# A float32 two-stack kernel: the S5 preparation cut into fine pieces, and the mixer's rotations and outputs placed elsewhere

## The chip, the core and the metric

The kernel runs on one core of a Trainium2 chip. The metric is the device time of the program in microseconds (us), from one launch; lower is better. Five engines of the core matter here: PE (TensorE, matrix products, results in PSUM), DVE (VectorE, elementwise work), ACT (ScalarE, activations, casts and copies), POOL (GpSimd, a second elementwise engine that also issues some DMAs) and SP (SyncE, which issues most DMAs). Each engine works through its own list of instructions in the order of that list.

## The reference

The input is one sequence of 256 positions of width 1024. A first stack has two layers, a second stack (attention, a dense feed-forward part, attention again, a mixture of experts) follows; the change touches only the first. Of that:

```python
h = x
for i in range(2):
    f = swiglu(rmsnorm(h, ...), ffn1_w_gate[i], ffn1_w_up[i], ffn1_w_down[i])
    h = h + 0.5 * rmsnorm(f, ...)
    m = mixer(rmsnorm(h, ...), ...);  h = h + rmsnorm(m, ...)
    ...                                    # ffn2, of the form of ffn1

def s5_branch(u, ...):                     # a part of the mixer
    lam_bar = jnp.exp(lam * step)          # 64 groups x 64 states, complex
    b_bar = ((lam_bar - 1.0) / lam)[..., None] * lax.complex(b_re, b_im)
    bu = jnp.einsum("blgc,gnc->blgn", ug, b_bar)
    # states[t] = lam_bar * states[t-1] + bu[t]
    y = jnp.real(jnp.einsum("blgn,gcn->blgc", states, c)) + d_skip * u
    val, gate = jnp.split(jax.nn.gelu(y) @ w_glu, 2, axis=-1)
    return val * jax.nn.sigmoid(gate)
```

The mixer projects its input with one wide matrix, sends parts of the result through a chunked state-space branch (SSD) and through the S5 branch, gates both, adds them and projects again. `swiglu` is `(silu(x @ w_gate) * (x @ w_up)) @ w_down` with a hidden width of 2816. All is float32.

## The kernel before

**Weights.** Every weight matrix is streamed from HBM in tiles of 128 x 1024 float32, called units here (512 KB each). SP issues the load into one of four raw buffers; ACT casts the tile to a rounded float32 form, `hi` (line 1576); DVE takes the difference `lo` (line 1577, "the split"); PE then makes three products for each pair of blocks: hi with hi, hi with lo, lo with hi (lines 1585 to 1593). The pairs of `hi` and `lo` rotate through a ring of three, lengthened in some stages by space that is free there (named `big`, `part` and `more` in the profile). `stream_b` keeps the weight block in the array and streams 256 positions (24 matmuls of 256 columns for a unit), `stream_k` keeps the input and streams 512 columns of the weights (12 matmuls for a unit). A feed-forward part has 66 units: six column blocks, c0 to c5, each with its gate and its up units, then 22 units of the down product, d0 to d21. The first block goes through `lead_b`, which runs its first five splits without waiting for the norm.

**Order of the work.** A tile scheduler decides each engine's list from its own estimates of time. The author binds it in places with `issue_after(x)`, which puts an instruction behind `x` on the engine of `x`. `self.last_lo` is the last split (on DVE), `self.last_mm` the last product of a unit (on PE), `self.last_pow` the reciprocal root of a norm (on POOL).

**The S5 preparation** runs beside ffn1, as a generator (`prep`) that is advanced at named places. It computes the step, the exponentials, sines and cosines of the recurrence (`mix_prep`, layer 0 only, some hundred DVE instructions on 128 x 64), a table of coefficients FL, then for each of four quarters q: POOL multiplies the input matrix B by powers (`s5_wb`, lines 341 to 344), DVE multiplies C by FL (`s5_ct`, lines 372 to 377, result s5CF), PE, ACT and DVE make the block matrices of the recurrence within four positions (`s5_products`, lines 396 to 414, PSUM tile zfa). For each half of 16 groups `s5_powers_prep` builds a table of 63 powers of a complex number by doubling (lines 301 to 303): for n = 1, 2, 4, ..., 32 two pairs of products, a difference and a sum, each on 16 groups x min(n, 63 - n) elements. In layer 0 both halves are built in ffn1; those of layer 1 are built in ffn2 of layer 0, at the units d2 and d8. The table `PREP` names the places at which the generator is advanced (its first list) and the products are made (its second), by column blocks c and down units d; each advance is bound behind the last split and behind the last norm's root.

**The mixer** (`mixer_body`) works through the list `ORDER`: p0 to p3 are four projection groups (eight units each, with a short convolution on DVE, line 569), d the step sizes of SSD (a chain of some 35 DVE instructions on 32 x 256, lines 585 to 604), g0 to g3 gates (four units each, accga to accgd), c0 to c3 the SSD cores, o0 to o3 the S5 outputs: 48 small matmuls (zoa to zod), then on ACT and DVE the gelu (`s5_gelu`, lines 504 to 509, and 515 to 559). Behind ORDER come the S5 gated product (`glu`, accgl), which needs all four outputs, and the two branch products. The S5 recurrence itself (`s5_rec`) rotates the states by the table of powers, scans them and rotates them back, for two halves of the groups: 14 DVE steps for a half (12 products, differences and sums of 128 x 1024, line 545, and two scans, line 549), 28 in all. It is `self.side`; `beside()`, which `stream_b` calls behind each split, advances it by one step. All 28 must be through before o0. The tables of the second half are loaded into the buffers of the first.

Of the kernel before, what the change touches and what calls it, by code (L numbers as in the profile page):

```python
# [30 lines left out]
ORDER = "p0 d p1 g0 g1 o0 o1 p2 c0 g2 c1 p3 o2 o3 g3 c2 c3".split()  # L31
# [4 lines left out]
    "X": [2, 3, 0, 1], "U": [4, 5], "A": [12, 13, 6, 7, 8, 9, 10, 11, 12, 13, 6, 7, 8, 9, 6, 7], "M": [15, 16],  # L36
# [42 lines left out]
class Mixer:  # L79
# [58 lines left out]
    def mix_prep(self, I):  # L138
# [67 lines left out]
        mag = self.exp32(cut, xr, P, NL)  # L206
        sn, cs = self.sincos32(cut, th, NL)

# [25 lines left out]
        cmul(*L[2], L[1], L[1])  # L234
        cmul(*L[3], L[2], L[1])
        cmul(*L[4], L[2], L[2])

# [6 lines left out]
        v.tensor_scalar_mul(lin, lim, -1.0)  # L244
        cmul(*f, (num, L[1][1]), (lre, lin))
        v.tensor_tensor(f[0], f[0], den, op=ALU.mult)
        v.tensor_tensor(f[1], f[1], den, op=ALU.mult)

        self.FL = ct.tile([P, 3, 4, NL], F32, name="FL")
        fi = t("fli")  # L250
        for d in range(4):
# [7 lines left out]
            v.tensor_scalar_mul(self.FL[:, 2, d, :], self.FL[:, 0, d, :], -1.0)  # L259

# [3 lines left out]
        cmul(*u2, (cs, sn), (cs, sn))  # L264
        cmul(self.s4dir[:, 0], self.s4dir[:, 1], u2, u2)
        v.tensor_tensor(mag, mag, mag, op=ALU.mult)
        v.tensor_tensor(self.s4len, mag, mag, op=ALU.mult)

# [12 lines left out]
    def s5_powers_prep(self, l, h):  # L281


        g = self.nc.gpsimd
        tt = self.nc.vector.tensor_tensor
        Ed = self.Ed[l, h] = self.dram.tile([3, P, 1024], F32, tag="Ed", name=self.nm("Ed"), bufs=4)
        if True:
            E = [self.slot("B", "E").rearrange("p (a i) -> p a i", i=64) for _ in range(3)]
            Et = self.slot("B", "Et").rearrange("p (k a i) -> p k a i", k=2, i=32)
            x, y = Et[:, 0], Et[:, 1]  # L290
            ls = slice(l * 32 + h * 16, l * 32 + h * 16 + 16)
            g.memset(E[2][:, :, 0], 0.0)
            self.nc.scalar.copy(E[2][:, :, 1:], self.s4len[:, ls].unsqueeze(2).to_broadcast([P, 16, 63]))
            for r in range(2):
# [9 lines left out]
            for r in range(3):  # L304
                g.dma_start(Ed[r], E[r].rearrange("p a i -> p (a i)"))
# [1683 lines left out]
```

## Time and profile before

| quantity | value |
|---|---|
| device time of three runs | 2931.49, 2934.55, 2935.66 us (median 2934.55) |
| profiled execution | time 2936.55 us, span 2934.5 us |
| mean granted PE clock | 0.981 of full speed |
| busy over the span | PE 2814.3 us (96%), DVE 2181.6 (74%), ACT 1674.2 (57%), POOL 206.0 (7%) |
| ffn1, mixer and ffn2 of layer 0 (accumulators) | 11.9 to 240.7, 247.7 to 662.5, 663.8 to 852.6 us |
| ffn1 and mixer of layer 1 | 855.3 to 1056.6, 1059.8 to 1473.8 us |

The profile is of one execution, 2.0 us above the median of the three runs. The span is the time from its first to its last instruction; all stages follow one another, because each needs the hidden state of the one before. A busy PE is not a PE at its peak, so each stage has to be read with its granted clock. Idle time of an engine is put down to whatever released it last.

### The profile page before, as it was taken

How to read it: one execution, taken by the hardware profiler on the slowest of the kernel's cores; microseconds unless marked ns; L12 is line 12 of the kernel's file. 1: busy time of each engine (PE TensorE's matmuls, PEld its weight loads, DVE VectorE, ACT ScalarE, POOL GpSimd, SP SyncE). 2: the span in 40 equal slices, each digit the busy share in tenths (PEclk: the TensorE clock that was granted, in tenths of full speed). 3: DMA queues.
4: the chain of work that ended last, by engine and by line, in shares of the span. 5: the costliest groups of instructions: out<-in, count | busy, mean ns of one | idle time of the engine just before them, and what ended most of it. 6: DMA issues, size and time to landing. Idle time of an engine off the chain costs nothing. (4 is left out here: it accounts for less than half of the span.)

```text
span 2934.5 us, 49144 instructions
## 1 busy us (share of the span) xinstructions
PE 2814.3 (96%) x19040; PEld 2508.2 (85%) x19040; DVE 2181.6 (74%) x3043; ACT 1674.2 (57%) x2389; POOL 206.0 (7%) x257
## 2 busy tenths in 40 slices
PE   8979999999999999999999999999999999999997
PEld 7968888999979888888999898987678888888886
DVE  5886877765667758777755566555589999999997
ACT  5434456545445444475554445445377777777776
POOL 2140001000004100010000000000000000000000
PEclk9999999999999999999999999999899999999998
DMA  7677565576567775656855646654589999999993
GB/s 238 199 250 242 160 204 164 197 227 188 184 223 249 241 221 174 194 155 196 264 171 180 215 154 192 186 192 132 184 279 356 343 361 361 343 359 356 354 344 145
DMA packets 350928, 687.88 MB, mean 234 GB/s; under 512 B 32672, under 2 KB 121952, under 8 KB 350688
## 3 DMA queue, kind: packets, MB, share of 16 engines
q1 hardware_dynamic: 336592, 637.42, 65.9%
q0 software_dynamic: 13952, 46.74, 4.8%
q8 instruction: 151, 2.47, 0.3%
q14 instruction: 89, 0.73, 0.1%
q10 hardware_dynamic: 144, 0.52, 0.0%
HBM read 658.05 MB, written 26.54 MB: 233 GB/s over the span
## 5 line engine op out<-in xcount | busy, mean ns | idle before, releaser
L1577 DVE TENSOR_TENSOR lo<-raw,hi 128x1024 fp32r<-128x1024 f32 x646 | 788.6, 1230 | 296.8 <-ACT hi L1576 285.1
L1576 ACT CAST hi<-raw 128x1024 fp32r<-128x1024 f32 x646 | 674.9, 1048 | 455.6 <-PE accmo L1587 84.6
L1586 PE MATMUL accmo<-lo,xg 128*128 128x512 f32 (+1 forms) x768 | 289.7, 378 | 2.3 <-DVE lo L1577 2.3
L1587 PE MATMUL accmo<-hi,xg 128*128 128x512 f32 (+1 forms) x768 | 285.2, 372 | 0.0
L1585 PE MATMUL accmo<-hi,xg 128*128 128x512 f32 (+1 forms) x768 | 274.0, 373 | 1.4 <-ACT hi L1576 1.4
L1577 DVE TENSOR_TENSOR big<-raw,big 128x1024 fp32r<-128x1024 f32 x147 | 184.9, 1259 | 110.2 <-ACT big L1576 109.3
L1576 ACT CAST big<-raw 128x1024 fp32r<-128x1024 f32 x147 | 153.7, 1049 | 168.0 <-issue 31.1
L1577 DVE TENSOR_TENSOR part<-raw,part 128x1024 fp32r<-128x1024 f32 x111 | 135.3, 1223 | 85.5 <-ACT part L1576 83.1
L1576 ACT CAST part<-raw 128x1024 fp32r<-128x1024 f32 x111 | 116.1, 1050 | 114.2 <-DMA raw<-in_ffn_w_gate_dram 17.4
L1586 PEld LDWEIGHTS accmo<-lo,xg 128*128 128x128 f32 x768 | 144.6, 188 | 32.3 <-DVE lo L1577 5.6
L1585 PEld LDWEIGHTS accmo<-hi,xg 128*128 128x128 f32 x768 | 144.6, 188 | 28.1 <-ACT hi L1576 2.6
L1587 PEld LDWEIGHTS accmo<-hi,xg 128*128 128x128 f32 x768 | 144.8, 189 | 22.5
L1586 PE MATMUL accmo<-lo,th 128*128 128x512 f32 x352 | 138.0, 392 | 0.0
L1587 PE MATMUL accmo<-hi,th 128*128 128x512 f32 x352 | 137.7, 391 | 0.0
L1577 DVE TENSOR_TENSOR lo<-big,hi 128x1024 fp32r<-128x1024 f32 x88 | 106.6, 1223 | 10.7 <-ACT hi L1576 7.6
L1585 PE MATMUL accmo<-hi,th 128*128 128x512 f32 x352 | 109.2, 391 | 0.0
L1576 ACT CAST hi<-big 128x1024 fp32r<-128x1024 f32 x88 | 92.7, 1054 | 27.0 <-PE accmo L1587 26.7
L1592 PE MATMUL accfa<-xh,lo 128*128 128x256 f32 x352 | 99.8, 284 | 0.0
L1591 PE MATMUL accfa<-xh,hi 128*128 128x256 f32 x352 | 99.7, 283 | 0.0
L1593 PE MATMUL accfa<-xl,hi 128*128 128x256 f32 x352 | 99.7, 284 | 0.0
L1577 DVE TENSOR_TENSOR lo<-more,hi 128x1024 fp32r<-128x1024 f32 x68 | 82.3, 1223 | 7.0 <-ACT hi L1576 5.0
L1576 ACT CAST hi<-more 128x1024 fp32r<-128x1024 f32 x68 | 71.4, 1053 | 19.3 <-PE accmo L1587 17.8
(993 smaller groups left out, 8603.3 us busy)
## 6 DMA issues: line engine op xcount, KB each, us to landing
raw<-in_w_gu_moe_dram SPq DMA_DIRECT2D x190, 512.0 KB, 5.3
raw<-in_w_in_dram SPq DMA_DIRECT2D x128, 512.0 KB, 4.4
raw<-in_w_down_moe_dram SPq DMA_DIRECT2D x94, 512.0 KB, 5.6
raw<-in_ffn_w_gate_dram SPq DMA_DIRECT2D x88, 512.0 KB, 4.1
raw<-in_ffn_w_up_dram SPq DMA_DIRECT2D x88, 512.0 KB, 4.3
raw<-in_ffn_w_down_dram SPq DMA_DIRECT2D x88, 512.0 KB, 4.2
big<-in_w_gu_moe_dram SPq DMA_DIRECT2D x60, 512.0 KB, 5.7
more<-in_w_gu_moe_dram SPq DMA_DIRECT2D x46, 512.0 KB, 5.7
```

The costliest lines, as they stand in the source:

```text
L1576: nc.scalar.copy(hi, raw)
L1577: self.last_lo = nc.vector.tensor_tensor(lo, raw, hi.bitcast(F32), op=ALU.subtract).ins
L1585: mm(ps, lh, rh, start=first, stop=False)
L1586: mm(ps, lh, rl, start=False, stop=False)
L1587: self.last_mm = mm(ps, ll, rh, start=False, stop=last).ins
L1591: mm(ps, lh, rh, start=first, stop=False)
L1592: mm(ps, ll, rh, start=False, stop=False)
L1593: self.last_mm = mm(ps, lh, rl, start=False, stop=last).ins
```

## The change

1. `PREP`, `product` and the binding to `last_pow` are gone. ffn1 sets `self.side = self.prep(...)` behind its first column block (layer 0) or its second (layer 1), and `beside()` advances it by one piece behind every split; `stream_k` now calls `beside()` too. The generator has many more yields: 48 pieces in layer 0 and 31 in layer 1, behind 58 and 50 splits. The rest, if there is any, runs at the end of the stage.
2. `s5_powers_prep` is called once for a layer, in ffn1 of that layer (layer 1 leaves ffn2). It builds 32 powers for all 32 groups of the layer, and ACT then copies them into tables for each half, whose middle is the power zero: once as they are, once reversed with the sign of the imaginary part turned. The first product by `jm` in `s5_products` moves from DVE to ACT.
3. In the mixer, `proj` sets `pace` to 2 except in p2, so that a rotation follows every second split there. ORDER puts p2 and g2 ahead of o0, g3 between c0 and c1. The lists of buffers X and A serve the new order.

```diff
-ORDER = "p0 d p1 g0 g1 o0 o1 p2 c0 g2 c1 p3 o2 o3 g3 c2 c3".split()
+ORDER = "p0 d p1 g0 g1 p2 g2 o0 o1 c0 g3 c1 p3 o2 o3 c2 c3".split()
 MIXER = {
-    "X": [2, 3, 0, 1], "U": [4, 5], ...
+    "X": [2, 3, 0, 1, 0] + [2, 3, 1, 0] * 5, "U": [4, 5], ...
...
-PREP = (
-    ("c0 c1 c2 c3 c4 d0 d3 d6 d9 d12".split(), "d0 d4 d10 d15".split()),
-    ("c1 c2 c4 d1 d6".split(), "c4 d1 d6 d11".split()),
-)
...
-    def s5_powers_prep(self, l, h):
+    def s5_powers_prep(self, l):
+        E = [self.slot("B", "E").rearrange("p (a i) -> p a i", i=32) for _ in range(2)]
...
+        for n in (1, 2, 4, 8, 16):
+            k = min(n, 31 - n)
+            b = [e[:, :, n : n + 1].to_broadcast([P, 32, k]) for e in E]
+            for r, op in ((0, ALU.subtract), (1, ALU.add)):
+                tt(x[:, :, :k], E[0][:, :, 1 : k + 1], b[r], op=ALU.mult)
+                if n > 8:
+                    yield
+                tt(y[:, :, :k], E[1][:, :, 1 : k + 1], b[1 - r], op=ALU.mult)
+                tt(E[r][:, :, n + 1 : n + 1 + k], x[:, :, :k], y[:, :, :k], op=op)
...
+        for h in range(2):
+            F = [self.slot("B", "Eh").rearrange("p (a i) -> p a i", i=64) for _ in range(3)]
+            for r in range(2):
+                g.memset(F[r][:, :, 0], 0.0)
+                cp(F[r][:, :, 32:], E[r][:, hs])
+                self.nc.scalar.activation(F[r][:, :, 1:32], E[r][:, hs, :0:-1], AF.Copy, scale=1.0 - 2.0 * r)
...
     def s5_products(self, q, p0, bq, CF, s):
-        nc.vector.tensor_scalar_mul(T, K, self.jm[:, 0:1])
+        nc.scalar.activation(T, K, AF.Copy, scale=self.jm[:, 0:1])
...
     def beside(self):
+        self.beat += 1
+        if self.beat % self.pace:
+            return
         with self.tc.issue_after(self.last_lo):
             next(self.side, None)
...
         def proj(g):
+            self.pace = 1 if g == 2 else 2
             pr[g] = self.ssd_proj(W, l, g, xh, xl)
+            self.pace = 1
...
     def stream_k(self, w, xh, xl, nk, order=None, aside=None):
             u = self.unit(w[k0 * P : (k0 + kk) * P, :], kk, D)
+            self.beside()
...
-                if aside:
-                    aside(f"d{i}")
...
     def ffn1(self, I, l, xT):
         def aside(w):
             if w == f"c{l}":
                 self.ring_drop((6, 7), (8, 9))
-            if w in at[1]:
-                self.product()
-            if w in at[0]:
-                with self.tc.issue_after(self.last_lo), self.tc.issue_after(self.last_pow.ins):
-                    next(steps, None)
+                self.side = self.prep(I, l)
```

DVE's list at the very start of the program, before (`big` and `lo` are splits, `xn` is the normed first half of the input, `xl` the low part of its transpose, `sm` a sum of the norm):

```order
L1747 SCALAR_TENSOR_TENSOR sm_122<-sm_116,sm_119 128x1
L1771 SCALAR_TENSOR_TENSOR xn_126<-h_99,sm_123,gn_114 128x512 x2
L1747 SCALAR_TENSOR_TENSOR sm_149<-sm_143,sm_146 128x1
L1771 SCALAR_TENSOR_TENSOR xn_153<-h_100,sm_150,gn_114 128x512 x2
L1577 TENSOR_TENSOR big_170<-raw_177,big_170 128x1024
L1720 TENSOR_TENSOR xl_113<-tr_128,xh_112 128x4x128
```

The same place after the change:

```order
L1775 SCALAR_TENSOR_TENSOR sm_122<-sm_116,sm_119 128x1
L1606 TENSOR_TENSOR big_170<-raw_177,big_170 128x1024
L1606 TENSOR_TENSOR big_170<-raw_187,big_170 128x1024
L1606 TENSOR_TENSOR lo_199<-raw_197,hi_198 128x1024
L1606 TENSOR_TENSOR lo_211<-raw_209,hi_210 128x1024
L1799 SCALAR_TENSOR_TENSOR xn_126<-h_99,sm_123,gn_114 128x512 x2
L1606 TENSOR_TENSOR lo_225<-raw_223,hi_224 128x1024
```

Four splits have moved ahead of the first normed half, and a fifth ahead of the second one. On ACT, the fifth cast (`hi_224`) likewise stands ahead of the squares of the second half and of every cast of a transposed input. On POOL, 14 DMA issues of the preparation, seven of which wait for earlier DMAs to land, have moved ahead of the first root of the norm.

DVE's list in the down product of ffn1, layer 0, before (L301 to L303 powers, L372 to L377 C times FL, L404 to L414 products):

```order
L410 TENSOR_TENSOR s5u_1607<-s5u_1607,dd_1802 128x8x16
L374 TENSOR_TENSOR s5CF_1827<-s5CF_1827,s5u_1828 128x8x64
L303 TENSOR_TENSOR E_1889<-Et_1892 128x16x8
L412 TENSOR_SCALAR s5u_1607<-s5u_1607,jm 128x512
L404 TENSOR_TENSOR dd_1990<-delta,sd 128x128
L376 TENSOR_TENSOR s5u_1828<-s5c_1602,FL 128x512
L1577 TENSOR_TENSOR big_170<-raw_2018,big_170 128x1024
```

The products of the first quarter after the change:

```order
L1606 TENSOR_TENSOR big_170<-raw_1905,big_170 128x1024
L426 TENSOR_TENSOR dd_1943<-delta,sd 128x128
L436 SCALAR_TENSOR_TENSOR s5u_1552<-s5u_1552,jm 128x8x48
L436 SCALAR_TENSOR_TENSOR s5u_1552<-s5u_1552,jm 128x8x32
L1606 TENSOR_TENSOR big_170<-raw_1965,big_170 128x1024
L388 TENSOR_TENSOR s5CF_1780<-s5c_1547,FL 128x8x64
L392 TENSOR_TENSOR s5CF_1780<-s5c_1547,FL 128x8x64
L436 SCALAR_TENSOR_TENSOR s5u_1552<-s5u_1552,jm 128x8x16
L1606 TENSOR_TENSOR lo_2002<-raw_2000,hi_2001 128x1024
```

Up to twelve instructions of three different strands stood between two splits before; now two or three stand there.

PE's list at the end of the last S5 output in the mixer of layer 0 (zod), before:

```order
L494 MATMUL zod_5344<-s5T_5341,U_3158 64x4x16
L495 MATMUL zod_5344<-s5CF_5340,S_2763 64x4x16
L496 MATMUL zod_5344<-s5CF_5340,S_2763 64x4x16
L1591 MATMUL accgd_5415<-xh_2478,hi_5420 128x256
L1592 MATMUL accgd_5415<-xh_2478,lo_5421 128x256
```

And after:

```order
L516 MATMUL zod_5442<-s5T_5439,U_3125 64x4x16
L517 MATMUL zod_5442<-s5CF_5438,S_2730 64x4x16
L518 MATMUL zod_5442<-s5CF_5438,S_2730 64x4x16
L1620 MATMUL accgl_5754<-g_632_4547,hi_5757 128x256
L1621 MATMUL accgl_5754<-g_632_4547,lo_5758 128x256
```

The 96 matmuls of the gate g3 (accgd) that stood behind zod have moved ahead of it, to the first outputs; the gated product accgl follows at once. It begins with the outputs 0 and 1; 48 of its matmuls stand ahead of the first transpose of output 2 in both lists.

## Rows read from the trace of the kernel before

**Rows 1.** The page, busy time of each engine over the span.

```profile
PE 2814.3 (96%) x19040; PEld 2508.2 (85%) x19040; DVE 2181.6 (74%) x3043; ACT 1674.2 (57%) x2389; POOL 206.0 (7%) x257
```

**Rows 2.** Stages: length; busy PE, PEld, DVE, ACT, POOL; granted clock; DMA.

```profile
12.00:100.00 88.00, 86.63 (x611) 81.48 (x611) 60.96 (x134) 47.87 (x66) 12.12 (x25) 1.00 0.71 218
100.00:246.00 146.00, 122.35 (x905) 107.36 (x904) 127.82 (x250) 56.00 (x78) 51.60 (x47) 0.94 0.76 243
...
337.00:402.00 65.00, 55.39 (x407) 53.84 (x406) 61.57 (x83) 24.71 (x38) 3.06 (x6) 0.89 0.59 189
...
476.00:530.00 54.00, 48.07 (x506) 42.85 (x504) 37.62 (x66) 34.93 (x70) 6.02 (x7) 0.97 0.42 134
...
663.00:853.00 190.00, 189.38 (x1258) 174.47 (x1257) 123.08 (x191) 93.04 (x129) 7.34 (x18) 1.00 0.66 205
853.00:1058.00 205.00, 200.17 (x1509) 182.59 (x1506) 140.50 (x165) 97.85 (x137) 51.68 (x40) 0.99 0.73 233
```

**Rows 3.** Waits of PE, 100 to 246 us: total, times, longest.

```profile
PE zfa L396 <- DVE s5CF L374: 7.5, 1, 7.5
PE trfa L1730 <- DVE xn L1771: 5.2, 1, 5.2
PE accfa L1586 <- DVE lo L1577: 4.4, 1, 4.4
PE accfa L1591 <- DVE ht L1827: 2.8, 1, 2.8
```

**Rows 4.** Waits of PE, 337 to 402 us (p1, g0, g1 of layer 0).

```profile
PE accgb L1592 <- DVE lo L1577: 3.2, 2, 2.3
PE accpb L1592 <- DVE lo L1577: 2.6, 1, 2.6
PE accga L1591 <- ACT zs L642: 2.3, 1, 2.3
```

**Rows 5.** DVE, busy time of the powers alone (tile Et), 12 to 246 us.

```profile
12.00:246.00 234.00, 29.69 (x72) 0.96 0.74 233
```

**Rows 6.** DVE by shape, 100 to 246 us: busy, mean ns, idle before.

```profile
L375 DVE TENSOR_TENSOR s5CF<-s5c,FL 128x512 f32<-128x512 f32 x4 | 5.0, 1240 | 0.0
...
L376 DVE TENSOR_TENSOR s5u<-s5c,FL 128x512 f32<-128x512 f32 x4 | 2.7, 682 | 0.0
...
L412 DVE TENSOR_SCALAR s5u<-s5u,jm 128x512 f32<-128x512 f32 x4 | 1.9, 479 | 0.0
```

**Rows 7.** The start, instructions in order of time: start us, us.

```profile
9.90 1.05 ACT L1576 CAST big<-raw 128x1024 fp32r<-128x1024 f32 x1 [1.47 <-DMA raw<-in_ffn_w_gate_dram]
...
11.93 0.79 PE L1585 MATMUL accfa<-big,xh 128*128 128x512 f32 x1
...
14.07 5.57 SPq L1571 DMA_DIRECT2D raw<-in_ffn_w_up_dram  x4
...
17.45 2.92 POOL L199 DMA_DIRECT2D sd<-in_s_d_dram  x6 [1.49 <-DMA cw<-in_conv_w_dram]
...
19.72 1.05 ACT L1576 CAST hi<-raw 128x1024 fp32r<-128x1024 f32 x1 [0.29 <-DMA raw<-in_ffn_w_up_dram]
...
20.17 0.39 PE L1587 MATMUL accfa<-big,xl 128*128 128x512 f32 x1
```

**Rows 8.** DVE by shape, 337 to 402 us.

```profile
L1577 DVE TENSOR_TENSOR lo<-raw,hi 128x1024 fp32r<-128x1024 f32 x13 | 15.6, 1206 | 1.5 <-ACT hi L1576 1.5
L545 DVE TENSOR_TENSOR S<-S,s5E 128x1024 f32<-128x1024 f32 x6 | 7.2, 1213 | 0.0
...
L549 DVE TENSOR_TENSOR_SCAN S<-s5E,S 128x1024 f32<-128x1024 f32 x2 | 4.6, 2277 | 0.0
```

**Rows 9.** Waits of PE, 476 to 530 us.

```profile
PE trod L515 <- DVE g L559: 1.2, 1, 1.2
```

**Rows 10.** The gelu of the last output (zod): start us, us.

```profile
490.74 0.57 ACT L504 COPY y<-zod 128x512 f32<-128x512 f32 x1
...
496.71 0.68 DVE L509 SCALAR_TENSOR_TENSOR y<-y 128x512 f32<-128x512 f32 x1
```

More of the change, by code (lines that the diff above doesn't have):

```diff
@@ L234, in mix_prep @@
         cmul(*L[2], L[1], L[1])
+        yield
         cmul(*L[3], L[2], L[1])
+        yield
         cmul(*L[4], L[2], L[2])
+        yield
         den, num, lin, f = t("den"), t("num"), t("lin"), (t("fr"), t("fi"))
@@ new lines, in s5_powers_prep @@
+        for h in range(2):
+            Ed = self.Ed[l, h] = self.dram.tile([3, P, 1024], F32, tag="Ed", name=self.nm("Ed"), bufs=4)
+            hs = slice(h * 16, h * 16 + 16)
+            F = [self.slot("B", "Eh").rearrange("p (a i) -> p a i", i=64) for _ in range(3)]
+            for r in range(2):
+                g.memset(F[r][:, :, 0], 0.0)
+                cp(F[r][:, :, 32:], E[r][:, hs])
+                self.nc.scalar.activation(F[r][:, :, 1:32], E[r][:, hs, :0:-1], AF.Copy, scale=1.0 - 2.0 * r)
+            g.memset(F[2][:, :, 0], 0.0)
+            ls = slice(l * 32 + h * 16, l * 32 + h * 16 + 16)
+            cp(F[2][:, :, 1:], self.s4len[:, ls].unsqueeze(2).to_broadcast([P, 16, 63]))
@@ L312, in s5_prep @@
         cb = [self.s5_cb(I, l, 0)]
-        yield
+        yield from self.s5_powers_prep(l)
         for q in range(4):
@@ L317, in s5_prep @@
                 cb.append(self.s5_cb(I, l, q + 1))
-            self.late.append(self.s5_ct(l, q, *cb.pop(0)))
-            yield
-            if l == 0 and q in (1, 2):
-                self.s5_powers_prep(0, q - 1)
-                yield
+            yield from self.s5_ct(l, q, *cb.pop(0))
     def s5_wb(self, I, l, q):
@@ L383, in s5_ct @@
             )
-        return lambda: self.s5_products(q, p0, bq, CF, s)
+        yield
+        yield
+        with self.tc.issue_after(self.last_mm):
+            self.s5_products(q, p0, bq, CF, s)
+        yield
     def s5_products(self, q, p0, bq, CF, s):
@@ L1431, in __init__ @@
         self.side = iter(())
+        self.beat, self.pace = 0, 1
         self.Ed = {}
@@ L1842, in ffn1 @@
         w = [I[f"ffn1_w_{k}"][l] for k in ("gate", "up", "down")]
-        steps = self.prep(I, l)
-        at = PREP[l]
         def aside(w):
@@ L1849, in aside @@
                 self.ring_drop((6, 7), (8, 9))
-            if w in at[1]:
-                self.product()
-            if w in at[0]:
-                with self.tc.issue_after(self.last_lo), self.tc.issue_after(self.last_pow.ins):
-                    next(steps, None)
-        return self.swiglu(*xT, *w, aside)()
+                self.side = self.prep(I, l)
+        banks = self.swiglu(*xT, *w, aside)()
+        for _ in self.side:
+            pass
+        return banks
     def ffn2(self, I, l, xT):
@@ L1868, in aside @@
                 self.mem_load(I)
-            if l == 0 and w in ("d2", "d8"):
-                with self.tc.issue_after(self.last_lo):
-                    self.s5_powers_prep(1, "d2 d8".split().index(w))
         return self.swiglu(*xT, *w, aside)()
@@ L1887, in prep @@
         yield from self.s5_prep(I, l)
-    def product(self):
-        with self.tc.issue_after(self.last_mm):
-            self.late.pop(0)()
     def first_body(self, I, h):
```

41 lines of the change are left out of this document (22 added, 19 removed).

## The prediction

> **What bounds the kernel now.** I read the page first: PE is busy 96% of the span [rows 1], so the change can only pay where PE idles or runs at the lower clock. The table of stages shows where [rows 2]. The feed-forward part of 663 to 853 us takes 190 us for its 66 units, with PE busy 189.4 and the clock at 1.00: that is the price of 66 units without disturbance, 2.88 us for each. The same 66 units of layer 0's ffn1 take 234 us (12 to 246). Layer 1's ffn1 takes 205 us, of which 4.8 are idle (205.0 less 200.2), so the S5 products that PE itself makes there cost about 10. In layer 0 then 234 - 190 - 10 = 34 us are lost; PE's idle time there is 1.4 + 23.6 = 25, and the rest, 9, is the lower clock that follows the waits (granted 0.94 on average over 146 us). In the waits of that stretch the first releaser is DVE every time [rows 3], and DVE is busy 127.8 of 146 us. In each mixer the same picture stands once more, from p1 to g1: 9.6 us of 65 idle, granted clock 0.89, DVE busy 61.6 of 65 [rows 2]. The waits name splits, and ACT's zs, whose products were late for the same reason [rows 4]. So DVE's list is what ends last in two kinds of place, and elsewhere PE is the bound.
>
> **ffn1 of layer 0.** Removed: the powers cost DVE 29.7 us there in 72 instructions [rows 5]. Before, the two halves build 62 powers x 16 groups each, 1984 elements; after, 30 x 32 = 960, in 30 instructions. By elements 14.4 us remain, so about 15 leave DVE (12 to 17, as one counts elements or instructions). The first product by jm goes to ACT, 4 x 0.48 = 1.9 [rows 6]; ACT is busy 56 of 146 us there and hides it, as it hides the copies into the tables. Moved: 48 pieces behind 48 splits. PE needs 48 x 2.88 + 10 = 148 us for that stretch. DVE had 61.0 + 127.8 = 188.8 us in the whole stage; less 17, less the 18 splits outside the stretch (18 x 1.2 = 22) and about 10 for the norms at both ends, 140 are left for it. That is 95% of PE's time: enough, with little to spare, and a piece is now two or three instructions where up to twelve stood between two splits. Of the 34 us the closing norm's wait stays, 5.2 [rows 3], with some 2 of low clock behind it, and the 1.4 at the start. That leaves 25 to win; since DVE is so nearly full, I take 17 (8 to 25). What would be late next is POOL, of which below.
>
> **The start.** Nothing binds the preparation to the norm's root any more. DVE does four splits before the first normed half, and ACT's fifth cast stands ahead of the squares of the second half and of every cast of a transposed input. That cast needs the first up tile. Its load can be issued when the first split has freed a buffer: first cast 9.90 to 10.95, split 1.2, so 12.2; the load took 5.65 us (issued 14.07, landed 19.72) [rows 7], so 17.8; the cast 18.9; then two squares and the cast of the transposed input, 1.5 to 3 us. The first product starts near 21 instead of 11.93. POOL's 14 DMA issues delay the root too: six took 2.92, so all some 7, half of them behind a landing of 5 to 6 us; that ends by 13 or 14 and hides behind the casts. Against this, PE did only eleven products of 512 columns up to 20.17 [rows 7], and was at full pace from there (twelve in 2.88 us, 0.24 each); at that pace it would have begun at 17.5. The loss is 3.4 us, plus 1 for eight transposes that were through by then, plus a new stretch at the low clock: half of a stretch that lasts 3 to 9 us. I take +7 (3 to 10).
>
> **Layer 1's ffn1 and layer 0's ffn2.** The first gets some 14 us of powers on a DVE that is busy 140.5 of 205 us, in small pieces, and loses its blocks: -1.5 (-4 to +3). The second loses them, but its PE was busy 189.4 of 190 us, so the gain is nought: the other units hid them.
>
> **The mixers.** Behind p0 and p1 every second split carries a rotation. By code, 25 of the 28 steps stood before o0 up to the end of g1, and now 17: six products and two scans fewer, 6 x 1.14 + 2 x 2.28 = 11.4 us of DVE [rows 8], against 9.6 us of idle PE and at most 65 x 0.11 = 7 of clock, 16.8 together. They return in p2 and g2. In p2 PE needs 8 x 2.88 = 23 us and DVE 8 splits, 8 steps with two scans and the convolution, about 26: 3 are lost again. The chain of the step sizes still runs in a block of some 10 us without a split, which the ring of three covers only in part: 2 to 3. I take -11 for each mixer (-17 to -4). The second half's tables are loaded when the first half's last product has read them; DVE has about 12 us of other work before it reads them, so this costs nothing, and if that cover went, all splits behind the waiting product would be late by what is missing.
>
> **The outputs.** With g3 gone from behind o3, the gelu of o3 has less to hide it. It took 6.65 us from the copy to the last product (490.74 to 497.39) [rows 10]; PE has 48 products of accgl, some 5.8 us, before it wants the transposes of o2, and twelve more before those of o3. Core c1's work stands among the gelu's instructions on DVE and ACT, which can double it. Below, the wait that stood there already, 1.2 [rows 9], may just stay: 0; above, 13.3 less 5.8, plus the clock: 11. I take +4 for each mixer, nearer to the single chain. The gate g3 itself hides the first outputs' chains at its new place.
>
> **Sum.** +7 - 17 - 1.5 + 0 + 2 x (-11 + 4) = -25.5 us. Against the profiled execution's 2936.55 that is 2911; the median of the runs is 2 us lower, 2934.55, so 2909.
>
> **Rivals.** First, POOL. The same product of 128 x 512 took 1240 ns on the mean at line 375 and 682 at line 376 [rows 6], in a stage where POOL is busy 51.6 us; DVE is slowed beside POOL's work on B, which the change leaves as it is. A split that is slowed so is late whatever stands around it. Then of ffn1's gain the lo and ht waits stay, 4.4 + 2.8 [rows 3], with 1.8 of clock: 9 less, 2918. For it: the size of the slowing. Against: the largest wait, 7.5, is for a chain of three strands, not for one slowed instruction. The Trainium skill (GPSIMD Engine Reference, "Key points") says that GpSimd "shares its SBUF interfaces with VectorE" and contends with DVE instructions that have two SBUF inputs; a split has two, so by that rule it would be slowed too, and the trace's 1240 against 682 agrees. By it the sum is this rival's.
>
> Second, the outputs cost the bound's 11 and somewhat more, 14 in each mixer instead of 4: -25.5 + 20 = -5.5, 2929, which is within 0.2% of before.
>
> Third, the other side: the glu start becomes a bound of its own. The gated product starts while o3's chain stands behind the whole of c1 on DVE, its weight splits stand behind that in the same list, and PE falls to the low clock. From 16.75 us in each mixer (4 + 25.5 / 2) nothing is gained; at 24 the sum is +14.5, 2949. For it: the splits of accgl do stand among c1's instructions. Against: g3's 96 products are not lost but done earlier, and the region's idle time was 5.9 of 54 [rows 2].
>
> Fourth, more than I take: DVE's surplus vanishes and the waits with it, ffn1 -22, mixers -15, outputs +2: about -40 to -45, near 2892.
>
> **How the numbers follow.** The forecast 0.60, POOL 0.17, more gained 0.09, the outputs 0.08, the glu start 0.06. A measurement of this kernel can tell about 0.2%, 5.9 us, from no change. Faster: 0.60 + 0.17 + 0.09 = 0.86; within: 0.08; slower: 0.06. The forecast's own bounds, added where they are independent, reach some 12 us to each side. The range goes from 2889, into the case of more, to 2929, the second rival.
>
> **What would show it.** In the profile after: the first product near 21 us; no zfa wait of several us and a ffn1 of layer 0 that ends 8 to 12 us earlier in net; powers that cost DVE about 14 us a layer; p1 to g1 at a clock near 1.00 with 2 to 5 us idle; waits of the o2 and o3 transposes for the gelu of 2 to 8 us in each mixer. Wrong it would be if PE waited for splits through all of ffn1 (DVE still full), or if the start cost 15 us, as it would when the second half's norm stood still longer behind the casts.

## The result, and the profile after

| | before | after |
|---|---|---|
| median | 2933.45 us (2931.49 to 2935.66) | 2972.26 us (2969.20 to 2976.72) |
| profiled execution, span | 2934.5 us | 2966.8 us |
| granted PE clock, mean | 0.981 | 0.976 |

The change makes the kernel slower: ratio 1.0135, 95% interval 1.0121 to 1.0150. The prediction said faster, 2909. The profiled executions differ by 32.3 us; that is the difference to be explained, and its parts are below. The page of after, busy time, against [rows 1]:

```profile
PE 2824.4 (95%) x19040; PEld 2518.2 (85%) x19040; DVE 2166.7 (73%) x2951; ACT 1688.3 (57%) x2409; POOL 208.8 (7%) x261
```

PE has the same 19040 products; DVE has 15 us less work, and yet the end is later. Stages of after, in the columns of [rows 2]: the start, ffn1 of layer 0, p1 to g1, the glu start, ffn2, ffn1 of layer 1.

```profile
12.00:22.00 10.00, 2.40 (x9) 2.00 (x10) 6.92 (x9) 6.37 (x11) 5.33 (x11) 1.00 1.05 389
...
100.00:247.00 147.00, 130.43 (x972) 115.67 (x970) 114.71 (x160) 66.34 (x95) 56.16 (x48) 0.93 0.79 258
331.00:398.00 67.00, 60.15 (x475) 59.23 (x473) 64.62 (x84) 27.90 (x43) 3.16 (x6) 0.95 0.69 213
470.00:534.00 64.00, 47.86 (x434) 43.04 (x435) 36.52 (x73) 32.60 (x65) 9.76 (x12) 0.77 0.26 83
678.00:868.00 190.00, 188.90 (x1255) 174.06 (x1253) 103.39 (x117) 90.58 (x121) 3.38 (x6) 1.00 0.62 188
869.00:1080.00 211.00, 201.82 (x1504) 183.99 (x1504) 152.10 (x191) 104.06 (x149) 53.96 (x53) 0.98 0.74 240
```

At the glu start PE is idle for 16 of 64 us and the clock is 0.77; before it was 5.9 of 54 at 0.97. ffn1 of layer 1 has 9 us idle instead of 5. The table takes the stages from the first product of one accumulator to the first of the next.

| stage | predicted | before | after | difference |
|---|---|---|---|---|
| start to the first accfa | +7 | 11.93 | 21.57 | +9.6 |
| ffn1 of layer 0, accumulators | -17 | 228.8 | 213.3 | -15.5 |
| its closing norm | 0 | 7.0 | 12.2 | +5.2 |
| mixers, accpa to accpc | -11 each | 96.7, 96.7 | 87.1, 86.5 | -9.7, -10.2 |
| mixers, accpc to accmb | +4 each | 164.5, 165.2 | 190.5, 180.5 | +26.0, +15.3 |
| ffn2 of layer 0 | 0 | 191.5 | 191.4 | -0.1 |
| ffn1 of layer 1 | -1.5 | 204.5 | 212.8 | +8.2 |
| all else, second stack +4.5 included | 0 | | | +3.4 |

The gains came, nearly in the size foretold. What failed is on the other side of the sum: the outputs, layer 1 and the closing norm. The first row is the shift of the first product; the prediction's 7 is a net loss, from which PE's faster work behind it is taken off (more of that below).

**The start.** After, in order of time (start us, us, engine, line, operation, idle before and releaser):

```profile
17.30 1.44 DVE L1799 SCALAR_TENSOR_TENSOR xn<-h,sm,gn 128x512 f32<-128x512 f32 x2
18.14 1.97 PE L1758 MATMUL tr<-ident,xn 128*128 128x128 f32 x8 [18.14 <-DVE xn L1799]
18.77 1.05 ACT L1605 CAST hi<-raw 128x1024 fp32r<-128x1024 f32 x1 [2.63 <-DMA raw<-in_ffn_w_up_dram]
...
20.95 1.05 ACT L1747 CAST xh<-tr 128x512 fp32r<-128x512 f32 x2
21.57 0.79 PE L1614 MATMUL accfa<-big,xh 128*128 128x512 f32 x1 [1.47 <-ACT xh L1747]
```

It is the chain that the prediction followed: the fifth cast waits for the up tile, and the input's cast stands behind it.

**The glu start.** PE after, at core c1's norm, and the same norm before; then POOL's two steps of the norm in after and before:

```profile
508.02 0.66 PE L721 MATMUL trcb<-M,xdt 128*64 128x256 f32 x4 [0.61 <-DVE M L716]
...
509.88 0.28 PE L1622 MATMUL accgl<-g,hi 128*128 128x256 f32 x1
519.48 1.01 PE L741 MATMUL trcb<-ones,zs 128*128 128x1 f32 x4 [9.32 <-POOL zs L739]
521.96 0.77 PE L751 MATMUL trcb<-dg,ones 128*128 128x128 f32 x2 [1.47 <-DVE dg L750]
...
517.37 2.06 POOL L739 TENSOR_TENSOR zs<-zs 128x512 f32<-128x512 f32 x2 [12.27 <-ACT zs L736]
```

```profile
492.20 0.66 PE L695 MATMUL trcb<-M,xdt 128*64 128x256 f32 x4
...
505.51 0.53 PE L715 MATMUL trcb<-ones,zs 128*128 128x1 f32 x4
...
503.20 2.18 POOL L713 TENSOR_TENSOR zs<-zs 128x512 f32<-128x512 f32 x2 [14.27 <-ACT zs L710]
```

From the core's last products to the product of its norm the way over DVE, ACT and POOL takes 11 to 13 us in both (508.0 to 519.5; 492.2 to 505.5). Before, 83 products of accgd (g3) and accgl stand between the two in PE's list; after, nine, and PE waits 9.3. This wait is not the whole loss: from g0 to the end of the gated product PE is idle for 23.7 us after (365 to 581 us, clock 0.92) and 11.3 before (370 to 566 us, clock 0.97).

### The profile page after: what moved, and what is told of

Same layout as the page of the kernel before. It is cut to its first block, busy times and chain, and to the rows that moved or that the text cites. A ratio compares the mean times of both kernels' runs of the same rounds, so it can differ in the third digit from the quotient of the medians.

```text
span 2966.8 us, 49077 instructions
## 1 busy us (share of the span) xinstructions
PE 2824.4 (95%) x19040; PEld 2518.2 (85%) x19040; DVE 2166.7 (73%) x2951; ACT 1688.3 (57%) x2409; POOL 208.8 (7%) x261
## 5 line engine op out<-in xcount | busy, mean ns | idle before, releaser
L1776 POOL TENSOR_TENSOR sm<-sm,mhalf 128x1 f32<-128x1 f32 x32 | 20.9, 654 | 1041.0 <-DVE sm L1775 1040.9
```

The lines of the kernel that those rows point to most:

```text
L1776: self.last_pow = nc.gpsimd.tensor_tensor(r, v, self.mhalf, op=ALU.pow)
```

## Which part of the change

The experiments are numbered e1 to e16 (there is no e8), and each is shown by its edit. e1 to e4 take the change apart. e1 binds the pieces behind the norm's root again:

```diff
-        with self.tc.issue_after(self.last_lo):
+        with self.tc.issue_after(self.last_lo), self.tc.issue_after(self.last_pow.ins):
             next(self.side, None)
```

> The changed kernel, with each piece of the side work bound behind the last norm's reciprocal root on POOL again, as well as behind the last split. Theory (the start is lost because nothing holds the preparation's DMA issues and memset behind the first root): the first product starts near 12 us instead of 21.6 and the whole is 8 to 10 us shorter than the changed kernel's 2972, about 2963. Rival (the early splits only shift the wait: DVE and POOL have the preparation to do anyway, and ffn1 is late again at its end): the first product is early, but the end of ffn1 stays near 247 us and the whole is within 3 us of 2972.

Measured 2957.44 (2955.93 to 2958.10), ratio 1.0083, more than was expected. The first product is at 11.32 us again; the stages of ffn1 stay within 3 us of after. The medians differ by 15 us, the profiled executions by 11: 10 at the start, and stages that differ both ways (layer 0's mixer 7 us shorter, ffn1 and mixer of layer 1 together 6 longer). e2, e3 and e4 lack this line; the later ones have it, all but e15.

e2 keeps the preparation and takes the mixer of before; e3 is the reverse, the kernel before with the new mixer alone:

```diff
-ORDER = "p0 d p1 g0 g1 p2 g2 o0 o1 c0 g3 c1 p3 o2 o3 c2 c3".split()
+ORDER = "p0 d p1 g0 g1 o0 o1 p2 c0 g2 c1 p3 o2 o3 g3 c2 c3".split()
-    "X": [2, 3, 0, 1, 0] + [2, 3, 1, 0] * 5, "U": [4, 5], ...
+    "X": [2, 3, 0, 1], "U": [4, 5], ...
         def proj(g):
-            self.pace = 1 if g == 2 else 2
```

> The changed kernel with the mixer of the kernel before: the old ORDER, the old list of X buffers and a rotation behind every split. Only the new preparation is left. Theory (losses are local to their stages): each mixer takes what it took before, 416.1 and 415.3 us from stage to stage, so 20 us come off the changed kernel, about 2952, and what stays over the kernel before (18) is the start, the closing norm of the first ffn1 (+5), layer 1's ffn1 (+8) and 4 in the second stack. Rival (the mixers are late because the new preparation leaves its tables late or in another place): the mixers stay at 421 to 430 us and the time near 2970.

> The kernel before with the changed mixer alone: new ORDER, new list of X buffers, a rotation behind every second split except in p2. Theory: both mixers lose what they lose in the changed kernel, 14 and 6 us, so about 2954; their first part, up to the end of g1, is 10 us shorter than before, and the gated product waits some 10 us for core c1's norm. Rival (the loss needs the new preparation): 2933 or less, by the 10 us that p1 to g1 gain in each mixer 2913.

Measured: e2 2943.82, ratio 1.0036 (1.0024 to 1.0049); e3 2961.73, ratio 1.0093 (1.0073 to 1.0113). Each missed its expected time by 8 us, in the sense that the mixer costs more: 28 and 29 us (2972.26 - 2943.82, 2961.73 - 2932.35), whichever preparation stands before it. The preparation costs 11, its start included.

e4 keeps the pace of 2 and takes the old ORDER and buffers:

> The changed kernel with the old ORDER and the old list of X buffers, but a rotation only behind every second split of p0, p1 and p3 as the change has it. Theory A (the new order is at fault: without g3 behind o3 nothing covers core c1's norm at the start of the gated product): the gain of p1 to g1 stays, 10 us in each mixer, and the loss at the gated product goes; against the same preparation with the old mixer (expected at 2952) some 15 to 20 us less, about 2934. Theory B (the rotations are at fault, since what p0 and p1 no longer do is done in p2 and p3, beside the outputs): mixers of 421 to 430 us as in the changed kernel, about 2972. In between: each takes a half.

Measured 2965.32, ratio 1.0107, nearer to theory B. accpa to accpc gains as foretold (87.2 and 90.9 us), accpc to accmb loses 13 and 21: in the old ORDER the pace pays and costs more than it pays. What it costs there is found below, with e12.

## What in the mixer

e7 is e1 with pace 1 and the new order. e9 is e1 (pace 2) with g3 back at its old place, between o3 and c2:

```diff
-            self.pace = 1 if g == 2 else 2
```

```diff
-ORDER = "p0 d p1 g0 g1 p2 g2 o0 o1 c0 g3 c1 p3 o2 o3 c2 c3".split()
+ORDER = "p0 d p1 g0 g1 p2 g2 o0 o1 c0 c1 p3 o2 o3 g3 c2 c3".split()
```

e10 and e11 have pace 1 and half of the new order each: e11 the list of e9 (p2 and g2 moved ahead of o0), e10 g3 alone moved, ahead of c1:

```diff
+ORDER = "p0 d p1 g0 g1 o0 o1 p2 c0 g2 g3 c1 p3 o2 o3 c2 c3".split()
```

> The changed kernel with the preparation held behind the norm's root and with the new ORDER, but a rotation behind every split again: 25 of the 28 steps stand before p2 instead of 17. Theory M (rotations moved into p2 and g2 make DVE late for the cores, and that is what the outputs and the gated product pay for): the stretch from g0 to the gated product falls back from 134 to about 129 us in layer 0 and the gated product from 75 to 80 down to 66; p1 to g1 lose their 5 us again; the whole about 2957 - 25 = 2932 to 2940. Theory O (g3 is missing behind o3, so nothing on PE covers core c1's norm): the gated product stays at 75 to 80 us in each mixer, the whole at 2955 to 2965.

> The changed kernel with the preparation held behind the norm's root, and g3 put back between o3 and c2, all else of the new ORDER and the pace kept. Theory O: the gated product's wait of 9 us for core c1's norm is covered by g3's 96 products again, the stretch of the gated product falls from 75 to 80 to about 65 us, 10 to 13 us in each mixer, the whole about 2934 to 2938. Theory M: the cores are late because of DVE; g3 only moves the wait from the gated product to g3 itself, the sum of the stretches from g0 to the branch product stays at 205 to 215 us in each mixer, the whole at 2950 to 2957.

> The changed kernel with the pieces of the preparation bound behind the norm's root, the old pace, and of the new order g3 alone (g3 stands before c1 instead of behind o3; p2 and g2 behind the outputs as before). Theory of the cover: between o0 and the last core the small work of outputs and cores must stand beside weight units; with g3 before c1, o2, o3, c2 and c3 have none left but the gated product. Then g3 to the mixer's end is longer by 10 to 16 us in each mixer, ga to mb 205 to 211 us instead of 195, and the time 2950 to 2960 (the version with the whole old mixer and the bound pieces took 2938). Rival: the loss comes from p2 and g2 standing ahead of o0; then ga to mb stays at 194 to 199 here, and the time is 2936 to 2942.

> As the other one, with g3 at its old place behind o3, and p2 and g2 ahead of o0, the old pace. Theory of the cover: the first outputs and the cores c0 and c1 have no weight unit between them from o0 to p3, so ga to gl grows by 8 to 16 us (140 to 147 us, where it was 130) and the stretch from gl to mb stays at 62 to 67; time 2950 to 2960. Rival (only g3's place matters): ga to mb at 194 to 199, time 2936 to 2942. If both kernels lose, the two losses together should come near the 14 to 18 us that the whole new order costs in each mixer; if their sum is far above it, they share one cause.

| | order | pace | accpa to accpc | accpc to accmb | median |
|---|---|---|---|---|---|
| e6 (below) | old | 1 | 95.2, 96.7 | 167.8, 165.4 | 2938.46 |
| e10 | g3 ahead | 1 | 98.8, 100.9 | 169.3, 165.4 | 2946.50 |
| e11 | p2, g2 ahead | 1 | 96.5, 95.0 | 179.4, 181.4 | 2962.69 |
| e7 | new | 1 | 97.1, 96.3 | 182.2, 184.1 | 2973.54 |
| e9 | p2, g2 ahead | 2 | 87.8, 90.3 | 181.0, 183.0 | 2958.59 |
| e1 | new | 2 | 87.7, 86.3 | 182.7, 185.4 | 2957.44 |

At pace 1, p2 and g2 cost 24 us and g3 8 (2962.69 and 2946.50 less 2938.46); their sum, 32, is near the 35 of both, so these are two losses and not one told twice. The theory of the cover held in e11 (its time 2.7 above the range). e10 came out between the two expectations: g3 alone is the small part. e7 lies above both of its expectations: with the new order, going back to pace 1 costs 16 us against e1, all of it ahead of accpc, and behind accpc nothing changes (182.2 and 184.1, 182.7 and 185.4). At pace 2 g3's place makes no difference (e9, e1): the wait moves from one core to another. PE's waits from accga to accmb, first e10, then e11, then e9:

```profile
PE trcb L741 <- POOL zs L739: 1.7, 1, 1.7
```

```profile
PE trca L741 <- POOL zs L739: 5.0, 1, 5.0
...
PE trca L751 <- DVE dg L750: 2.2, 1, 2.2
```

```profile
PE trca L741 <- POOL zs L739: 5.3, 1, 5.3
...
PE trca L751 <- DVE dg L750: 2.0, 1, 2.0
```

The releaser is POOL's sum each time, but POOL itself waited for the chain; `trca` is core c0, `trcb` c1. In before 24 units (p2, g2, p3, g3) stand between o0 and c2, in e11 and e9 12 (p3, g3), in after 12 (g3, p3). PE's lists show it more closely. Counted in all profiles of this case, in both layers and for all four cores: where 42 or more products of units stand between a core's last product and the product of its norm, PE waits there 0.4 us at most; in e10, with 30, 1.7 and 2.6; where none to ten stand there, 1.1 to 9.3.

e12 is e4 with the line of e1 and without the second half of the recurrence:

```diff
-        self.side = itertools.chain(self.s5_rec(St, l, 0, E), self.s5_rec(St, l, 1))
+        self.side = self.s5_rec(St, l, 0, E)
```

> Old order and old lists, pace 2, the preparation bound behind the root; the second half of the S5 recurrence is left out (14 of 28 steps, the outputs of that half are computed from states that were not rotated back). Theory of the moved rotations: pace 2 pushes eight steps, 11.4 us of DVE, into p2 and g2, where they stand among the outputs and the cores and make the cores late; without the second half nothing is pushed there, and ga to mb falls from 203 and 215 us to 195 or below in both mixers. Rival: the steps themselves cost nothing, what costs is a list that the scheduler orders in another way; then ga to mb stays above 203.

Measured 2921.61; accpa to accpc 91.0 and 90.8, accpc to accmb 159.7 and 163.6. With nothing pushed behind accpc, e4's loss there is gone. That alone would not tell the theory from its rival (the list that the scheduler orders in another way); the traces do. The load of the first output's coefficients (s5CF, mixer of layer 0), in before, e4 and e12:

```profile
401.61 0.54 POOL L482 DMA_DIRECT2D s5CF<-Td  x1 [6.69 <-DVE S L545]
```

```profile
424.54 0.53 POOL L504 DMA_DIRECT2D s5CF<-Td  x1 [34.32 <-DVE S L567]
```

```profile
374.55 0.53 POOL L504 DMA_DIRECT2D s5CF<-Td  x1 [2.85 <-ACT tg L779]
```

The load goes into a buffer that the recurrence uses for its intermediate results (number 2, in the lists X and W), and in before and e4 it follows the last of the 28 steps (which end at 401.32 and 424.24 us), in e12 the last of the 14 (374.02). At pace 2 that step comes behind units of p2 and g2. So in e4 PE's list has all 288 products of p2 and g2 ahead of the products of the first output that read the states (68 in before), as if the ORDER were the new one, and between core c0's last product and its norm no product of a unit is left (79 in before, 78 in e12). e4 loses the same cover as e11. That the steps cost anything by DVE's time is not shown, and in the new order pace 2 gains 16 us (e1 against e7). How much of e12's 160 is also due to less work in all was not separated.

## What in ffn1

e5 is e1 without POOL's four products of B in each quarter (a remnant of eight columns stays). e6 is e1 with the old mixer, and with layer 1's powers in ffn2 of layer 0:

```diff
-        tt(tv, Bv, lam(1), op=ALU.mult)
-        tt(Bv, Bv, lam(0), op=ALU.mult)
-        tt(Bv[:, 0], Bv[:, 0], tv[:, 1], op=ALU.subtract)
-        tt(Bv[:, 1], Bv[:, 1], tv[:, 0], op=ALU.add)
+        tt(tv[:, 0, 0, :8], Bv[:, 0, 0, :8], lam(0)[:, 0, 0, :8], op=ALU.mult)
+        tt(Bv[:, 0, 0, :8], Bv[:, 0, 0, :8], tv[:, 0, 0, :8], op=ALU.add)
```

```diff
-        yield from self.s5_powers_prep(l)
+        if l == 0:
+            yield from self.s5_powers_prep(0)
+        else:
+            yield
...
+            if l == 0 and w == "c3":
+                self.side = self.s5_powers_prep(1)
```

> The changed kernel with the preparation held behind the norm's root (as in the first experiment of that kind, 2957) and without POOL's four products of B with the powers, of which only an 8-column remnant stays in each quarter: that part of the S5 input matrix is left out. Theory (layer 1's ffn1 is 8 to 11 us longer because DVE's splits and pieces run 2.7 to 3.1 us instead of 1.2 to 1.8 beside those products): layer 1's ffn1 takes 205 to 207 us instead of 215.4, its ht waits of 3 us go, layer 0's ffn1 gives back its zfa waits and, since the preparation ends sooner, the closing norm's 5 us; in all 12 to 18 us, about 2942. Rival (the powers and the single pieces fill DVE there, POOL or not): ffn1 of layer 1 stays above 212 us and the whole within 4 us of 2957.

> The mixer of the kernel before (old ORDER, old X list, a rotation behind every split), the new preparation held behind the norm's root, and layer 1's powers made in layer 0's ffn2 again, in pieces behind its splits. Theory (each loss stands where it was found): the start as in the kernel before (first product near 11.5 us), the first mixer begins near 238 us instead of 247.7, ffn2 of layer 0 stays at 191.5 us, ffn1 of layer 1 falls from 213 by the powers' share, 2 to 4 us, to about 210, the mixers as before: 2933 - 10 + 5 = 2928. Rival (losses move on, as in the changed kernel): what the first ffn1 wins is lost in the mixer or in ffn2, 2933 or more.

Measured: e5 2926.85, 30.6 us below e1 and 15 below what was expected; ffn1 with its closing norm goes from 226.1 to 208.6 (layer 0) and from 215.4 to 201.7 (layer 1). e6 2938.46, ratio 1.0018, on the rival's side: without the powers ffn1 of layer 1 still takes 215.5, and ffn2 with them 191.4. So the powers are not layer 1's loss, and POOL's products are. The shape groups of DVE in after, 100 to 235 us (busy, mean ns, idle before), and below them e5's splits:

```profile
L1606 DVE TENSOR_TENSOR lo<-raw,hi 128x1024 fp32r<-128x1024 f32 x22 | 30.0, 1363 | 3.9 <-ACT hi L1605 3.9
L394 DVE TENSOR_TENSOR s5u<-s5c,FL 128x512 f32<-128x512 f32 x4 | 8.1, 2032 | 0.1
L391 DVE TENSOR_TENSOR s5CF<-s5CF,s5u 128x512 f32<-128x512 f32 x4 | 7.1, 1770 | 0.1
...
L392 DVE TENSOR_TENSOR s5CF<-s5c,FL 128x512 f32<-128x512 f32 x4 | 2.7, 684 | 0.0
```

```profile
L1604 DVE TENSOR_TENSOR lo<-raw,hi 128x1024 fp32r<-128x1024 f32 x24 | 29.1, 1220 | 4.0 <-ACT hi L1603 4.0
```

The same product takes 0.68 us alone and up to 2.0 on the mean beside POOL. Four kernels more tell what this is. e15 is the kernel before with one word changed:

```diff
     def s5_wb(self, I, l, q):
-        tt = nc.gpsimd.tensor_tensor
+        tt = nc.vector.tensor_tensor
```

e13 has the old mixer, e1's line, and the same word, with a `yield` around each of B's products so that it is a piece of its own. e14 is e13 with four products of the same sizes on POOL, for which nobody waits, and e16 is e13 with e6's second diff:

```diff
+        dm = self.slot("B", "dm").rearrange("p (r d n) -> p r d n", r=4, d=4)
+        pt = nc.gpsimd.tensor_tensor
+        pt(dm, fl[0], fl[1], op=ALU.mult)
+        pt(dm, dm, fl[2], op=ALU.mult)
+        pt(dm[:, :2], dm[:, :2], fl[0][:, :2], op=ALU.subtract)
+        pt(dm[:, 2:], dm[:, 2:], fl[1][:, 2:], op=ALU.add)
```

> The preparation of the change bound behind the root, the old mixer, and the four products of B on DVE, in pieces of their own, instead of POOL. Theory of POOL (its products slow DVE's work beside them, and are themselves late): each product costs DVE some 1.2 us, 16 of them 19 us in a stage, but no split is slowed any more and the closing norm does not wait for the last of them. ffn1 of layer 0 takes 209 to 216 us (226 with POOL, 209 without any product), that of layer 1 202 to 207 (215 and 202), the time is 2912 to 2922, below the kernel before. Rival (DVE is too full for them): 16 us more on a DVE that is the bound there come back in full, ffn1 of layer 0 takes 222 to 228, layer 1's 212 to 218, and the time stays at 2930 to 2940.

> The version with the old mixer and B's products on DVE, and beside each quarter's first product four products of the same sizes on POOL, on a buffer of their own whose result nobody reads. Theory of slowed DVE: POOL's work by itself makes DVE's two-operand instructions slow while it runs, so ffn1 of layer 0 goes from 214.9 back to 222 to 230 us and layer 1's from 203.2 to 210 to 217, and splits beside POOL take 2.5 to 3 us instead of 1.2; time 2930 to 2945. Rival, lateness: POOL only hurt because B's products came late for what waits for them; with nobody waiting, ffn1 stays at 213 to 218 and 202 to 206 us and the time at 2915 to 2922.

> The kernel before with one word changed: B's four products of each quarter on DVE instead of POOL, with the old coarse pieces. If POOL's slowing was a loss of the kernel before too, and the fine pieces are worth little, ffn1 of layer 0 falls from 235.8 to 217 to 226 us and layer 1's from 204.5 to 200 to 204, and the time is 2917 to 2928, near the 2916 of the fine pieces with the same products on DVE. If the fine pieces are what makes room for them, the products lengthen the blocks between two splits by 1.2 to 4.7 us each, and ffn1 of layer 0 stays at 230 to 240 us: time 2929 to 2940.

> The version with the old mixer and B's products on DVE, with layer 1's powers in ffn2 of layer 0, where 12 to 14 us of DVE stand idle beside 190 us of PE. With POOL's products the same move changed nothing. If DVE's surplus is now what ffn1 of layer 1 lacks, that stage falls from 203.2 to 199 to 201 us and the time to 2912 to 2914; if PE is its bound, it stays at 202 to 204, and the time at 2916.

| | ffn1 of layer 0, with its norm | of layer 1 | median | ratio to before |
|---|---|---|---|---|
| before | 235.8 | 204.5 | | |
| e6: fine pieces, POOL | 227.4 | 215.5 | 2938.46 | 1.0018 (1.0006 to 1.0030) |
| e13: fine pieces, DVE | 214.9 | 203.2 | 2916.39 | 0.9940 (0.9926 to 0.9954) |
| e14: e13 and idle POOL products | 225.9 | 210.9 | 2934.46 | 1.0003 (0.9993 to 1.0013) |
| e15: before, DVE | 216.1 | 203.2 | 2916.86 | 0.9944 (0.9923 to 0.9966) |
| e16: e13, powers of layer 1 in ffn2 | 216.4 | 201.9 | 2915.68 | 0.9932 (0.9911 to 0.9953) |

e13 beats both kernels, as the theory of POOL expected. From e6 to e13 the two stages fall by 12.5 and 12.3 us; in e14 POOL's work alone, with nobody waiting for its result, gives back 11.0 and 7.7 of them. So slowed DVE is the larger part, and what is left for late products, 1.5 and 4.6, the smaller. One thing e14 does not separate: POOL's DMA issues stand in its list behind the idle products (one of these took 5.89 us), so they are late as well. DVE and POOL in e14, in order of time:

```profile
131.86 2.42 POOL L366 TENSOR_TENSOR dm<-dm,FL 128x1024 f32<-128x1024 f32 x1
131.89 2.94 DVE L405 TENSOR_TENSOR s5CF<-s5CF,s5u 128x512 f32<-128x512 f32 x1
...
175.28 3.77 DVE L1622 TENSOR_TENSOR big<-raw,big 128x1024 fp32r<-128x1024 f32 x1
175.40 1.31 POOL L367 TENSOR_TENSOR dm<-dm,FL 128x512 f32<-128x512 f32 x1
176.66 1.30 POOL L368 TENSOR_TENSOR dm<-dm,FL 128x512 f32<-128x512 f32 x1
```

DVE's product ends 0.55 us after POOL's, having 0.68 of its own; the split takes 3.77, and 1.22 + 1.31 + 1.30 is 3.83. The two engines take turns.

e15 says most. The coarse pieces of before, with 16 products more on DVE, run as fast as the fine ones. The wait of 7.5 in [rows 3] and that of 4.4 are gone, and the product that took 1240 ns [rows 6] takes 683; e15, that product from 100 to 235 us, and PE's waits from 11 to 238 us:

```profile
L375 DVE TENSOR_TENSOR s5CF<-s5c,FL 128x512 f32<-128x512 f32 x4 | 2.7, 683 | 0.0
```

```profile
PE trfa L1730 <- DVE xn L1771: 6.0, 1, 6.0
PE zfa L396 <- DVE s5CF L377: 1.9, 1, 1.9
PE accfa L1586 <- DVE big L1577: 1.4, 1, 1.4
```

e16 is within e13's interval: with POOL out of the way, the place of layer 1's powers is worth 1.3 us of its stage and nothing measurable in all.

## Why the prediction was wrong, point by point

**What bounds ffn1.** That DVE's list ends last was right; that it does so because of coarse pieces was not shown by any row. The prediction had the row that tells (1240 against 682 ns, [rows 6]) and set it aside, because "the largest wait, 7.5, is for a chain of three strands, not for one slowed instruction". That is the first step that failed: a chain of three strands is late when its links are slow, and e15 takes the wait away without touching the pieces. The Trainium skill's rule on GpSimd and DVE (GPSIMD Engine Reference, "Key points"), cited there as a rival, is what all of e5 and e13 to e15 agree with; the rival's price, 9, was half of what the runs then gave (17.5 from e1 to e5, where the products are missing; 19.7 from before to e15).

**ffn1 of layer 0, -17.** Measured -15.5; against e1, which has the old start, 12.9 of it are ffn1's own (228.8 to 215.9). So the term was right within its range of 8 to 25. The powers cost DVE 10.09 us after, 29.69 before [rows 5], 19.6 less where 12 to 17 was taken. How much of the gain comes from the smaller powers and how much from the finer pieces was not separated. That the coarse pieces are the cause is not shown: e15 keeps them and gains more by one word, and without POOL's products fine pieces and smaller powers together are worth 1.2 us (216.1 in e15, 214.9 in e13).

**The closing norm, 0.** The prediction let it stay; it grew by 5.2. After, order of time:

```profile
216.63 7.07 POOL L357 TENSOR_TENSOR s5t<-s5B,s5L 128x1024 f32<-128x1024 f32 x1 [8.63 <-DMA s5B<-in_s_bT_dram]
...
229.67 0.56 POOL L441 DMA_DIRECT2D Td<-s5CF  x1
...
232.78 2.00 ACT L1605 CAST part<-raw 128x1024 fp32r<-128x1024 f32 x2 [6.56 <-DMA Td<-s5CF]
233.87 2.36 DVE L1606 TENSOR_TENSOR part<-raw,part 128x1024 fp32r<-128x1024 f32 x2 [5.29 <-ACT part L1605]
...
238.21 1.28 DVE L1809 TENSOR_TENSOR y<-accfa,gn 128x512 f32<-128x512 f32 x2
```

The last quarter of B is done late, and its first product takes 7.07 us beside three splits and two products on DVE (3.76 is the mean of its four). The store of s5CF stands behind it on POOL; the mixer's first split needs that buffer, and the closing norm stands behind the split on DVE. The prediction counted POOL's DMA issues at the start and none here. In e5, without the products, this gap is 4.0 us long, not 12.2. But POOL is not all of it: with the products on DVE it is 9.7 in e13 and 14.2 in e15, where pieces of the preparation still stand among DVE's steps of the norm. So a preparation that ends late, on whichever engine, is the likely reason; no run took it apart further.

**The start, +7.** The first product came 9.6 us later; the chain and its time (21 foretold, 21.57) were right. The prediction's 7 is the loss that is left at the end of the stage, and against e1 the accumulators end 7.7 later (234.90 and 227.17 us): right too. One part of it did not come: the new stretch at the low clock (granted 1.00 from 12 to 22 us).

**ffn1 of layer 1, -1.5 (-4 to +3).** Measured +8.2. The term costed the powers, which e6 and e16 show to cost next to nothing; it left out POOL, whose products cost this stage 12 to 14 us once the pieces are fine (215.5 in e6, 203.2 in e13, 201.7 in e5). After, DVE and POOL in layer 1:

```profile
937.55 2.68 DVE L1606 TENSOR_TENSOR lo<-raw,hi 128x1024 fp32r<-128x1024 f32 x1 [2.71 <-ACT hi L1605]
...
940.82 2.77 DVE L1606 TENSOR_TENSOR lo<-raw,hi 128x1024 fp32r<-128x1024 f32 x1
943.51 1.78 DVE L388 TENSOR_TENSOR s5CF<-s5c,FL 128x512 f32<-128x512 f32 x1
...
936.73 2.41 POOL L357 TENSOR_TENSOR s5t<-s5B,s5L 128x1024 f32<-128x1024 f32 x1
939.70 2.81 POOL L358 TENSOR_TENSOR s5B<-s5B,s5L 128x1024 f32<-128x1024 f32 x1
```

Two splits, with only 0.74 us of other work between them, take 2.7 us each; behind them in DVE's list stands an `ht`, for which PE waits 1.5 us at 947.4. Before, POOL did as much work there and slowed DVE too: DVE was busy 140.9 us, and 139.4 in e15 with 15.2 us of products more, so some 17 us were lost to POOL (an estimate from these three numbers). Yet the stage lost only 1.4 against e15's 203.2. Why the coarse pieces came off so lightly in this layer was not tried and stays open.

**The mixers, -11.** Measured -9.7 and -10.2 up to accpc: right. The prediction followed the moved steps only as DVE's time in p2 and g2. They also hold back o0, which stands behind the last of the 28 (the load rows above); so with pace 2 the units of p2 and g2 are through before o0 in either ORDER, and the gain here has its price in the next term.

**The outputs, +4 (0 to 11).** Measured +26.0 and +15.3. This is the term that turned the sign, and the step that failed: the sum has a price for the gelu of o3 and none for the cores' norms. It asked what g3 hid behind o3, and found the gelu of o3. By the rows above g3 hid core c1's norm, 12 us over three engines. And p2 and g2, whose place the prediction costed only by the rotations in them, hid more than g3 did (24 against 8 us, e11 and e10): core c0's norm, among others. The waits for c1's norm are 9 to 11 us in each mixer of after; how the rest of the loss divides between the lower clock and smaller waits was not worked out. The third rival, that the glu start becomes a bound of its own (2949, chance 0.06), is what happened, but through the core's norm, and not through o3's chain and the weight splits.

**The sum.** With the two terms as measured, 41 in place of 8, and layer 1's 8.2 in place of -1.5, the forecast's -25.5 becomes +17; the norm, the start and the scatter of the rest give the other 15. The range's upper end, 2929, was worked out from outputs of 14 at most.

## What to carry to other kernels

Before a unit of weights is moved, list every chain over several engines that runs beside it, the longest one first, and not only the neighbour in the order that comes to mind: here the norm of a core, 12 us without any work of PE of its own, was paid, 9.3 us of it, as soon as its cover left. Before steps are pushed to later, ask what stands behind the last of them: here a load that needed their buffer, and with it the whole first output. And where an engine is "full", look at the same instruction's duration in two places before cutting its list into finer pieces: two numbers, 1240 and 682 ns, held a gain of 17 us that one word brings.

## What the runs showed of the hardware

A two-operand product on DVE and one on POOL did not share time but took turns, in e14's rows to within 0.2 us: 3.77 for a split of 1.22 beside 2.61 of POOL. The Trainium skill (SBUF — State Buffer, "SBUF: two separate sides") calls the shared ports an exclusive lock for a whole instruction, and the rows agree. The engine that waits can be passed over more than once: the split waited for two products of POOL, and a product of POOL took 7.07 us, where 2.41 was the shortest, beside five instructions of DVE. Work moved from POOL to the busy DVE therefore cost DVE less than nothing: its 16 products take 15.2 us in e15, and yet its busy time in ffn1 of layer 0 with the closing norm falls from 190.48 to 175.72 us. Before, then e15:

```profile
12.00:247.70 235.70, 210.68 (x1521) 190.32 (x1521) 190.48 (x387) 104.45 (x144) 63.72 (x72) 0.96 0.74 235
```

```profile
11.20:227.30 216.10, 205.86 (x1521) 186.64 (x1520) 175.72 (x381) 103.10 (x143) 26.02 (x53) 0.98 0.79 253
```
